# Residuals of the last two layers' weight tiles: from GpSimd and VectorE to VectorE alone

## The chip, the cores and the metric

The kernel runs on one core of a Trainium2 chip. TensorE (PE) does the matrix products, VectorE (DVE), ScalarE (ACT) and GpSimd (POOL) work on tiles, SyncE (SP) issues most of the DMAs. The metric is the device time of one execution in microseconds. Each engine carries out its own instructions in order; an instruction waits on semaphores for what it needs from another engine or a DMA.

## The reference

The input x has 256 tokens of 1024 channels. A first block (16 meta tokens in front, sliding-window attention beside a state-space model, then a feed-forward layer of 16,384 one-neuron experts) is followed by two more layers, and those are what the change touches:

```
def even_layer(x, ln, w_in, qkn, lam, subln, w_out, layer):
    h = rmsnorm(x, ln)
    aq, ak, av, az, bq, bk, bv, bz = split_cols(h @ w_in, EVEN_SPLITS)
    oa = dilated_attention(rmsnorm(heads(aq)), rmsnorm(heads(ak)), heads(av), ...)
    ob = diff_attention(rmsnorm(bq), rmsnorm(bk), heads(bv), lam_f, ...)
    mixed = concatenate([oa * silu(az), rmsnorm(ob, subln) * (1 - lam_init) * silu(bz)])
    return x + mixed @ w_out

def odd_layer(x, ln, w_in, qkn, phi_pe, phi_w1, phi_w2, w_out):
    h = rmsnorm(x, ln)
    cq, ck, cv, cz, dq, dkc, dvc, dks, dvs, dkw, dvw, dz, dg = split_cols(h @ w_in, ODD_SPLITS)
    oc = moba_attention(rmsnorm(heads(cq)), rmsnorm(heads(ck)), heads(cv), ...)
    k_cmp = rmsnorm(compress_blocks(heads(dkc), phi_pe[0], phi_w1[0], phi_w2[0]))
    v_cmp = compress_blocks(heads(dvc), phi_pe[1], phi_w1[1], phi_w2[1])
    od = nsa_attention(rmsnorm(heads(dq)), k_cmp, v_cmp, ..., sigmoid(dg), ...)
    mixed = concatenate([oc * silu(cz), od * silu(dz)])
    return x + mixed @ w_out
```

All of it is in float32.

## The kernel before, in words

Every large product is made of three products of a shorter format (fp32r), so that little precision is lost (`mm3`): a weight tile w of 128x1024 is rounded to H, its residual is Lo = w - H, and the activations are split into xH and xL in the same way. L1702 multiplies xH by H, L1703 xH by Lo, L1704 xL by H, all three into the same PSUM bank (`pr` in the last two layers, `ps` before them).

The weight tiles of the whole kernel come through one object, `Feed`. For each unit it issues the load of w on SyncE (L89, five w buffers), the rounding to H as a copy on ScalarE (L102), and the residual as a subtraction (L103) on the engine that the unit's job list names; `eng[(2 * i + q) % len(eng)]` goes through that list in turn. It stays two, later three, units ahead of the one in use. The job lists of the last two layers, `we`, `woe`, `wod`, `wog` and `woo`, have 32 + 8 + 28 + 4 + 8 = 80 units, of 1024 columns but for the four of `wog`, which have 560. Before them, in the first block, the residuals are on VectorE, but for the four of `wu`, which are on GpSimd.

`even` (L1366) and `odd` (L1433) are one `Layer` each. `enter` transposes the activations, `group` makes one slice of the projection with 4 units, 16 k-steps and two halves of the tokens. What follows a slice is `heads` for queries and keys: a square (L1192, ScalarE), a sum per head (L1193), `rstd` (L1712 to L1720, some 15 small VectorE instructions, an integer start value and three Newton steps), the scaling (L1196, L1197, into qs), and later, on TensorE, the transposes of qs (L1203). Other slices are `values` (a scaled copy) or `swish`. `scores` multiplies queries by keys (L1295), takes them with their bias from PSUM (L1298) and makes the softmax; `weigh` transposes the probabilities S (L1334) and multiplies them by the values (L1340). In `even`, two score matrices are combined (L1402) and the result is normed per head (L1417 to L1423, emx). In `odd`, keys of two kinds are normed into kn (L1470 to L1475, transposed at L1482), and a small compression (X, Y, copied over partitions by DMA at L1578, then gathered into XS at L1588) gives kr (L1630, transposed at L1639). The projection runs as a background to the attention: its matmuls are handed out in steps between the attention's.

Which instruction stands where on an engine is decided by a scheduler, which plans the whole program by its own costs and writes each engine's order. A residual's engine is one of its inputs, so the diff of one line moves instructions on several engines.

Of the kernel before, what the change touches and what calls it, by code (L numbers as in the profile page):

```python
# [1642 lines left out]
def body(tc, A, out):  # L1643
# [3 lines left out]
    with ExitStack() as ctx:  # L1647
# [23 lines left out]
        def evac(dst, src):  # L1671
# [3 lines left out]
            else:  # L1675
# [2 lines left out]
        c.evac = evac  # L1678

        P, V = nc.gpsimd, nc.vector  # L1680
        LE = [P, P, V]
        jobs = [(A["wu"], 1024, [P]), (A["wkv"], 1024, [V]), (A["wq"], 1024, [V]), (A["wo"], 1024, [V]), (A["wqy"], 1024, [V]),
                (A["ut"], 1024, [V]), (A["pv"], 1024, [V]), (A["we"], 1024, LE), (A["woe"], 1024, LE), (A["wod"][:, :2], 1024, LE),
                (A["wog"], 560, LE), (A["wod"][:, 2:], 1024, LE), (A["woo"], 1024, LE)]

# [212 lines left out]
```

## Time and profile before

| what | us |
|---|---|
| median of 3 runs (1373.74 to 1376.59) | 1375.31 |
| the profiled execution | 1379.08 |
| its span | 1377.2 |
| PE busy in the span | 1283.5 (93%) |
| DVE busy | 930.7 (68%) |
| ACT busy | 648.4 (47%) |
| POOL busy | 424.0 (31%) |

The mean granted TensorE clock was 0.958 of full speed. The last two layers begin at about 1008 us of the span and run to its end. All times of rows are us from the start of the span unless marked ns. A gap of an engine is written behind its row as [idle before <- what ended it].

### The profile page before, as it was taken

What the parts mean: (1) busy time and instruction counts of PE and PEld (TensorE: products, weight loads), DVE (VectorE), ACT (ScalarE), POOL (GpSimd) and SP (SyncE); (2) the same over time, 40 slices, a digit from 0 to 9 for tenths busy, and PEclk for the clock granted to TensorE, in tenths of its full rate; (3) what the DMA queues carried; (4) which work ended last, traced back from release to release, by engine and by line L of the source; (5) the groups of instructions that cost most, each with busy time, mean ns of one, the idle gap of its engine ahead of it and who ended that gap; (6) DMA issues with size and microseconds to landing.
All of it is one profiled execution on the core that took longest, in us unless ns stands there. A gap on an engine that the chain in (4) does not pass through costs nothing.

```text
span 1377.2 us, 21248 instructions
## 1 busy us (share of the span) xinstructions
PE 1283.5 (93%) x7816; PEld 1107.7 (80%) x7816; DVE 930.7 (68%) x2137; ACT 648.4 (47%) x1119; POOL 424.0 (31%) x257
## 2 busy tenths in 40 slices
PE   4569899999999999998999999999998989979998
PEld 4455789999999999998887888888876768756777
DVE  6963469898898666664788855555567845585734
ACT  4424345544545444444544444544554545533552
POOL 7010000477788777600000000000043426431143
PEclk9877989999999999999999999999999979997999
DMA  5359255788887777897999865665664325551231
GB/s 200 61 61 369 76 185 174 207 229 220 234 221 209 194 208 200 250 368 245 300 305 309 301 192 188 186 193 187 186 219 131 123 79 166 196 164 50 77 107 61
DMA packets 106296, 262.75 MB, mean 191 GB/s; under 512 B 31552, under 2 KB 37056, under 8 KB 103888
## 3 DMA queue, kind: packets, MB, share of 16 engines
q1 hardware_dynamic: 75280, 227.77, 52.9%
q0 software_dynamic: 21696, 16.85, 6.6%
q10 hardware_dynamic: 9216, 16.78, 3.3%
q8 instruction: 61, 1.00, 0.3%
q14 instruction: 43, 0.35, 0.1%
HBM read 232.72 MB, written 28.38 MB: 190 GB/s over the span
## 4 chain that ended last, share of the span: by engine, by line
PE 74%; DVE 11%; DMA 6%; issue 2%; ACT 1%; SPq 0%; DVEq 0%; ACTq 0%
PE ps L890 22%; PE ps L1702 10%; PE ps L1703 10%; PE ps L1704 10%; PE pr L1702 4%; PE pr L1704 4%; PE pr L1703 4%; PE m L1295 2%; DVE Lo L103 2%; DMA glu<-in_glu 2%; PE ps L1103 2%; DMA ga<-ascr 2%; PE o L1340 1%; DMA T<-kdr 1%; DVE rs L1719 1%
## 5 line engine op out<-in xcount | busy, mean ns | idle before, releaser
L102 ACT CAST H<-w 128x1024 fp32r<-128x1024 f32 (+1 forms) x370 | 386.0, 1045 | 502.4 <-PE ps L1703 211.5
L103 DVE TENSOR_TENSOR Lo<-w,H 128x1024 fp32r<-128x1024 f32 x310 | 386.0, 1246 | 171.8 <-ACT H L102 171.7
L103 POOL TENSOR_TENSOR Lo<-w,H 128x1024 fp32r<-128x1024 f32 (+1 forms) x60 | 141.8, 2367 | 626.2 <-ACT H L102 619.5
L1061 POOL DMA_INDIRECT wscr<-sent x128 | 241.0, 1883 | 225.8 <-DVE act L1038 157.0
L1702 PE MATMUL ps<-xH,H 128*128 128x256 f32 x1024 | 290.8, 284 | 0.0
L1703 PE MATMUL ps<-xL,H 128*128 128x256 f32 x1024 | 287.8, 281 | 0.0
L1704 PE MATMUL ps<-xH,Lo 128*128 128x256 f32 x1024 | 287.6, 281 | 0.0
L890 PE MATMUL ps<-H,a 128*128 128x512 f32 x1024 | 281.8, 397 | 5.3 <-ACT a L902 3.0
L890 PEld LDWEIGHTS ps<-H,a 128*128 128x128 f32 x1024 | 194.0, 190 | 51.3 <-ACT a L902 3.2
L1702 PEld LDWEIGHTS ps<-xH,H 128*128 128x128 f32 x1024 | 193.1, 189 | 0.0
L1703 PEld LDWEIGHTS ps<-xL,H 128*128 128x128 f32 x1024 | 193.1, 189 | 0.0
L1704 PEld LDWEIGHTS ps<-xH,Lo 128*128 128x128 f32 x1024 | 193.0, 188 | 0.0
L890 PE MATMUL ps<-Lo,a 128*128 128x512 f32 x512 | 161.7, 397 | 0.9 <-DVE Lo L103 0.9
L890 PEld LDWEIGHTS ps<-Lo,a 128*128 128x128 f32 x512 | 96.8, 189 | 24.5 <-DVE Lo L103 1.9
L900 DVE TENSOR_TENSOR act<-ga,act 128x256 f32<-128x256 f32 x128 | 47.4, 420 | 26.0 <-DMA ga<-ascr 25.8
L1702 PE MATMUL pr<-H,exH 128*128 128x512 f32 x128 | 54.3, 425 | 0.9 <-ACT exH L1143 0.9
L1702 PE MATMUL pr<-H,oxH 128*128 128x512 f32 (+1 forms) x128 | 52.9, 416 | 1.1 <-ACT oxH L1143 1.1
L903 DVE TENSOR_TENSOR a<-act,a 128x256 fp32r<-128x256 f32 x128 | 53.5, 419 | 0.0
L902 ACT CAST a<-act 128x256 fp32r<-128x256 f32 x128 | 51.3, 401 | 3.1 <-DMA ascr<-ga 2.1
L1704 PE MATMUL pr<-H,oxL 128*128 128x512 f32 (+1 forms) x128 | 52.6, 411 | 0.0
L1704 PE MATMUL pr<-H,exL 128*128 128x512 f32 x128 | 52.5, 410 | 0.0
L1703 PE MATMUL pr<-Lo,oxH 128*128 128x512 f32 (+1 forms) x128 | 51.9, 406 | 0.4 <-DVE Lo L103 0.4
(493 smaller groups left out, 1956.7 us busy)
## 6 DMA issues: line engine op xcount, KB each, us to landing
w<-in_ut SPq DMA_DIRECT2D x128, 512.0 KB, 4.4
w<-in_pv SPq DMA_DIRECT2D x128, 512.0 KB, 4.3
ascr<-ga ACTq DMA_DIRECT2D x64, 256.0 KB, 3.0
ga<-ascr SPq DMA_DIRECT2D x64, 256.0 KB, 5.5
w<-in_we SPq DMA_DIRECT2D x32, 512.0 KB, 3.6
w<-in_wod SPq DMA_DIRECT2D x28, 512.0 KB, 3.7
wscr<-zero POOLq DMA_DIRECT2D x4, 2048.0 KB, 30.3
w<-in_wqy SPq DMA_DIRECT2D x16, 512.0 KB, 3.5
```

What stands on the lines that cost most here:

```text
L102: self.last = self.nc.scalar.copy(H, self.loaded[u])
L103: eng.tensor_sub(Lo, self.loaded[u], H.bitcast(FT))
L890: nc.tensor.matmul(acc[2 * th + n], a[:, s], b[:, n * 512:(n + 1) * 512], start=first and e == 0, stop=last and e == 2)
L900: V.tensor_tensor(src, ga[:, blk % 2], src, op=OP.mult)
L902: copied = nc.scalar.copy(aH, src)
L903: V.tensor_sub(aL, src, aH.bitcast(FT))
L1061: ins = c.nc.gpsimd.indirect_dma_start(out=c.wscr.rearrange("i b (t o) -> (i b t) o", o=1), out_offset=bass.IndirectOffsetOnAxis(ap=t.bitc ...
L1103: nc.tensor.matmul(p[:, a * 128:(a + 1) * 128], o1[:, a], o2[:, a], start=True, stop=True)
L1295: nc.tensor.matmul(sp[:, :off + nk], q(h)[:, ts], k(h)[:, :off + nk], start=True, stop=True)
L1702: nc.tensor.matmul(o, ah, bh, start=first, stop=False)
L1703: nc.tensor.matmul(o, ah, bl, start=False, stop=False)
L1704: nc.tensor.matmul(o, al, bh, start=False, stop=last)
```

## The change

In `body`, at L1681, the list of engines for the residuals of the last two layers is shortened from three entries to one:

```
         P, V = nc.gpsimd, nc.vector
-        LE = [P, P, V]
+        LE = [V]
         jobs = [(A["wu"], 1024, [P]), ...
                 (A["ut"], 1024, [V]), (A["pv"], 1024, [V]), (A["we"], 1024, LE), (A["woe"], 1024, LE), (A["wod"][:, :2], 1024, LE),
                 (A["wog"], 560, LE), (A["wod"][:, 2:], 1024, LE), (A["woo"], 1024, LE)]
```

Of the 80 residuals 56 change from GpSimd to VectorE, three of which have 560 columns; the 24 that VectorE had stay. GpSimd keeps the four of `wu` and its other work. The scheduler writes new orders. Three places on VectorE:

In the even layer's keys, `rstd` of the second `heads` (rs_10564, made from qs_10558), between the reduction L1193 and the scaling L1197:

```order
 L1718 TENSOR_TENSOR rs_10564<-rs_10564 128x16
 L1719 TENSOR_TENSOR rs_10564<-rs_10564 128x16
+L103 TENSOR_TENSOR Lo_10606<-w_10491,H_10605 128x1024
 L1720 SCALAR_TENSOR_TENSOR rs_10564<-rs_10564 128x16
 L1718 TENSOR_TENSOR rs_10564<-rs_10564 128x16
```

A residual that GpSimd did now stands within the chain.

In the even layer's last `heads` (qs_11025, qs_11026, rs_11031), beside the norm of the second half of the tokens (bss_10934, emx):

```order
+L1193 TENSOR_REDUCE hss_11024<-qs_11025 128x8
 L1421 SCALAR_TENSOR_TENSOR bss_10934<-rs_10941,st_10706 128x4
+L1193 TENSOR_REDUCE hss_11024<-qs_11026 128x8
 L1423 TENSOR_TENSOR emx_10280<-emx_10280,bss_10934 128x512
-L1193 TENSOR_REDUCE hss_11024<-qs_11025 128x8
-L1193 TENSOR_REDUCE hss_11024<-qs_11026 128x8
 L1712 TENSOR_SCALAR rs_11031<-hss_11024 128x16
+L103 TENSOR_TENSOR Lo_11055<-w_10912,H_11054 128x1024
 L1713 TENSOR_SCALAR ri_11032<-rs_11031 128x16
-L103 TENSOR_TENSOR Lo_11055<-w_10912,H_11054 128x1024
 L1714 TENSOR_SCALAR ri_11032<-ri_11032 128x16
 L1715 TENSOR_SCALAR rs_11031<-rs_11031 128x16
```

The two reductions are earlier by one instruction of the norm, and the residual by one of rstd.

In the odd layer, the gathers XS and the norm of its keys (kss_11932, kn_11933):

```order
+L103 TENSOR_TENSOR Lo_11861<-w_11703,H_11860 128x1024
+L103 TENSOR_TENSOR Lo_11879<-w_11709,H_11878 128x1024
 L1588 COPY XS0_11888<-X_11833 128x8x15 x4
-L1588 COPY XS1_11895<-X_11844 128x8x15 x2
 L103 TENSOR_TENSOR Lo_11911<-w_11795,H_11910 128x1024
-L1588 COPY XS1_11895<-X_11844 128x8x15 x2
+L1588 COPY XS1_11895<-X_11844 128x8x15 x4
 L1460 TENSOR_SCALAR gt_11692<-pr_11815,r_11646 128x24
 L1460 TENSOR_SCALAR gt_11692<-pr_11816,r_11646 128x24
 L1470 TENSOR_REDUCE kss_11932<-kn_11933 128x8
 L1462 TENSOR_SCALAR gt_11692<-gt_11692 128x48
+L103 TENSOR_TENSOR Lo_11963<-w_11817,H_11962 128x1024
```

Two residuals now stand ahead of the gathers and one behind kss; two more stand between it and kn. On SyncE one load of a `wod` tile now goes ahead of the X copies of L1578; on GpSimd no residual of these layers is left.

## Rows read from the trace of the kernel before

**Rows 1.** Windows: stretch, us; busy us (instructions) PE, PEld, DVE, ACT, POOL; PEclk; DMA; GB/s

```profile
1008.00:1377.00 369.00, 336.01 (x1665) 260.48 (x1664) 229.77 (x646) 174.63 (x362) 141.75 (x68) 0.93 0.38 123
1049.00:1056.00 7.00, 3.44 (x16) 2.56 (x14) 4.22 (x8) 1.21 (x3) 2.34 (x1) 0.76 0.51 150
1071.00:1109.00 38.00, 29.29 (x146) 23.89 (x146) 36.13 (x87) 15.67 (x20) 16.74 (x7) 0.97 0.40 130
1111.00:1126.00 15.00, 15.00 (x50) 10.32 (x51) 6.62 (x36) 6.50 (x27) 0.00 (x0) 0.56 0.09 24
1242.00:1268.00 26.00, 26.00 (x91) 16.95 (x90) 14.53 (x73) 11.41 (x40) 4.00 (x2) 0.64 0.07 22
1276.00:1302.00 26.00, 25.08 (x150) 20.00 (x149) 23.50 (x82) 15.44 (x43) 4.74 (x2) 1.00 0.26 78
```

**Rows 2.** Timeline of PE: start, us, engine, line, operation [idle before <- releaser]

```profile
1052.81 1.51 PE L1203 MATMUL m<-cstt,qs 128*128 128x128 f32 x6 [3.56 <-DVE qs L1197]
...
1074.83 0.44 PE L1334 MATMUL m<-cstt,S 128*128 128x128 f32 x2 [2.03 <-DVE S L1402]
...
1108.58 1.94 PE L1203 MATMUL m<-cstt,qs 128*128 128x128 f32 x8 [6.69 <-DVE qs L1197]
...
1219.07 1.16 PE L1482 MATMUL m<-cstt,kn 128*128 128x128 f32 x4 [5.39 <-DVE kn L1475]
...
1239.09 0.20 PE L1639 MATMUL m<-cstt,kr 16*128 16x16 f32 x1 [3.73 <-DVE kr L1630]
```

**Rows 3.** Views of single lines on DVE: ns min/median/max, first and last start

```profile
L1719 DVE TENSOR_TENSOR rs<-rs x39: 139/174/2412, 1020.1 to 1293.3; 128x16 f32<-128x16 f32 x21, 128x2 f32<-128x2 f32 x6, 128x4 f32<-128x4 f32 x6, 128x8 f32<-128x8 f32 x3
L1193 DVE TENSOR_REDUCE hss<-qs x14: 669/677/686, 1029.7 to 1289.2; 128x8 f32<-128x512 f32 x14
L1402 DVE SCALAR_TENSOR_TENSOR S<-S,st x8: 343/410/2585, 1064.3 to 1075.1; 128x128 f32<-128x128 f32 x4, 128x256 f32<-128x256 f32 x4
L1423 DVE TENSOR_TENSOR emx<-emx,bss x2: 691/1736/2782, 1082.9 to 1099.1; 128x512 f32<-128x512 f32 x2
L1588 DVE COPY XS<-X x8: 244/358/2469, 1203.8 to 1211.0; 128x120 f32<-128x120 f32 x8
```

**Rows 4.** Timelines of POOL and DVE at 1049 us, one row of each

```profile
1049.09 2.34 POOL L103 TENSOR_TENSOR Lo<-w,H 128x1024 fp32r<-128x1024 f32 x1 [0.45 <-DVE rs L1718]
...
1049.13 2.33 DVE L1719 TENSOR_TENSOR rs<-rs 128x16 f32<-128x16 f32 x1
```

**Rows 5.** Groups of L103: from 1006 us (two), to 1006 us; busy, mean ns | idle

```profile
L103 POOL TENSOR_TENSOR Lo<-w,H 128x1024 fp32r<-128x1024 f32 x53 | 128.1, 2422 | 618.1 <-ACT H L102 611.5 <-DVE rs L1715 3.5 <-DVE x L883 2.6
...
L103 DVE TENSOR_TENSOR Lo<-w,H 128x1024 fp32r<-128x1024 f32 x23 | 36.4, 1582 | 11.6 <-ACT H L102 11.6
...
L103 DVE TENSOR_TENSOR Lo<-w,H 128x1024 fp32r<-128x1024 f32 x286 | 348.9, 1221 | 158.6 <-ACT H L102 158.5
```

**Rows 6.** Timeline of DVE in 1071 to 1109 us

```profile
1079.13 2.24 DVE L1719 TENSOR_TENSOR rs<-rs 128x4 f32<-128x4 f32 x1
...
1084.78 1.29 DVE L1712 TENSOR_SCALAR rs<-hss 128x16 f32<-128x16 f32 x1
...
1090.47 2.54 DVE L103 TENSOR_TENSOR Lo<-w,H 128x1024 fp32r<-128x1024 f32 x1
```

**Rows 7.** Timeline of DVE in the odd layer

```profile
1203.79 5.93 DVE L1588 COPY XS<-X 128x120 f32<-128x120 f32 x6 [1.85 <-DMA X<-Y]
...
1215.22 2.26 DVE L1720 SCALAR_TENSOR_TENSOR rs<-rs,ri 128x8 f32<-128x8 f32 x1
...
1234.38 2.31 DVE L1718 TENSOR_TENSOR rs<-rs 16x2 f32<-16x2 f32 x1
...
1295.21 2.37 DVE L1196 TENSOR_SCALAR hss<-rs,r 128x8 f32<-128x8 f32 x1
```

**Rows 8.** DMA issues, the page's section 6

```profile
w<-in_wod SPq DMA_DIRECT2D x28, 512.0 KB, 3.7
```

**Rows 9.** Waits of DVE from 1006 us: total us, times, longest

```profile
DVE Lo L103 <- ACT H L102: 13.2, 11, 2.7
```

More of the change, by code (lines that the diff above doesn't have):

```diff
@@ L1680, in body @@
         P, V = nc.gpsimd, nc.vector
-        LE = [P, P, V]
+        LE = [V]
         jobs = [(A["wu"], 1024, [P]), (A["wkv"], 1024, [V]), (A["wq"], 1024, [V]), (A["wo"], 1024, [V]), (A["wqy"], 1024, [V]),
```

## The prediction

> **What bounds the kernel now.** I read first the windows of the last two layers [rows 1]. From 1008 us to the end TensorE is busy in 336.0 of 369 us and VectorE in 229.8, GpSimd in 141.8. TensorE sets the time, so an edit on VectorE or GpSimd can be worth only two things: TensorE's idle time, 33 us here, and the stretches in which its granted clock is at the lower of its two levels (1.2 instead of 2.4 GHz; mean 0.93). The next view is TensorE's timeline, to see who ends its idle time [rows 2]: the five large gaps sum to 21.4 us, and every one is ended by VectorE: by qs, S, kn, kr, each the last product of a chain of small dependent instructions (rstd, lines 1712 to 1720). Why are those chains long? The line views [rows 3] answer: the multiplication L1719 takes 0.14 to 0.17 us, but up to 2.41. The timelines of both engines side by side [rows 4] show when: GpSimd's residual runs from 1049.09 for 2.34 us, VectorE's L1719 from 1049.13 for 2.33 us, and they end together. The tensor_reduce L1193, 677 ns in the median, never stretches (669 to 686). I call a VectorE instruction that is held until GpSimd's residual ends a lock.
>
> The Trainium skill says the same in "SBUF — State Buffer", section "Who interferes with whom": the port pair that the two engines share is an exclusive lock, which a reduction never takes. Another page speaks against the change: "Perfetto Trace Analysis", section "Optimizing Scalar/DVE Operations", says that moving operations between these two engines might not help because of that port. By it the sum would be near zero; it is rival B, which is priced from rows below.
>
> **The change, part by part.** Of the 80 residuals Lo of the last two layers, 56 leave GpSimd: 53 of 128x1024 and three of 128x560. GpSimd took 2.42 us for one, VectorE takes 1.22 where GpSimd is quiet, 1.58 in the last layers [rows 5]. VectorE gets 53 x 1.22 = 64.7 us more, and three small ones of about 1.22 x 560/1024 = 0.67 (an estimate), 66.7 in all. It loses its own stretching: 23 x (1.58 - 1.22) = 8.3 us on its own residuals, and the locks on the rest. GpSimd keeps 15 - 3 = 12 small instructions, so a few locks may stay. The totals decide nothing, since VectorE, at most 229.8 + 66.7 = 296.5 of 369, has room on the whole; what counts is what stands in each chain that TensorE waits for. I went through the order of the changed kernel at each place, with the durations of before.
>
> - Keys of the even layer, gap 3.56 at 1052.81 [rows 2]. The chain holds two locks, of which one stands in [rows 4]: 2 x (2.4 - 0.17) = 4.4. In the changed order one more residual stands inside it (first place in the order): +1.2. Net -3.2; the gap can lose at most its 3.56. Bounds -3.6 and +1.2.
> - Softmax to the last heads, 1071 to 1109, gaps 2.03 and 6.69 [rows 2]. VectorE is busy 36.13 of 38 us with seven GpSimd residuals in the stretch [rows 1], so here every us on VectorE is a us for TensorE. Locks: L1402's longest 2.59 - 0.41, its median, = 2.17; L1719 2.24 - 0.17 = 2.07; L1712 1.29 - 0.17 = 1.12, and a like one of 0.88; L103 2.54 - 1.22 = 1.32 [rows 6]; L1423 2.78 - 0.69 = 2.09 [rows 3, 6]; one more of that kind on L1713, 2.08. Sum 11.7. Against it ten residuals stand where three did: 7 x 1.22 = 8.5. Net -3.2. Three more TensorE matmuls now stand ahead of the transposes; at 25.08/150 = 0.17 us each [rows 1] that fills another 0.5 of the gap. So -3.7. If VectorE had no locks to lose it would be +8.5, and no more than the 8.7 of the two gaps can go: bounds -8.7 and +8.5.
> - kn in the odd layer, gap 5.39 at 1219.07. Two locks, 2.26 and its like, are 4.2; six copies XS take 5.93 where the median copy takes 0.36, 3.7 more [rows 3, 7]. In front of kn stand now five more residuals (third place in the order): 6.1, of which two fit into the 1.85 us in which VectorE waited for X [rows 7]; two of 560 columns come before those, 1.3 in all, of which I count half, 0.7, between none and all. On SyncE one weight load now goes ahead of the X copies, which can make X late by at most the 3.7 us of such a load [rows 8]; loads run side by side on 16 engines, and I take 1.0. Net -7.9 + 6.1 - 1.9 + 0.7 + 1.0 = -2.0. Bounds -5.4, the gap itself, and -7.9 + 6.1 + 1.3 + 3.7 = +3.2.
> - kr, gap 3.73 at 1239.09. Two locks, one of them the 2.31 of [rows 7]: 4.2 less, one residual more: 1.2. kr's chain now also stands ahead of the q heads'. Net -2.8. Bounds -3.7 and +1.2.
> - Odd middle, 1240 to 1302. In 1276 to 1302 VectorE is busy 23.50 of 26 and TensorE 25.08 [rows 1]: the one place where TensorE doesn't wait yet and could. Eleven residuals stand where three did, +9.8; a lock of 2.37 [rows 7], 2.2 net, its like on L1712 and a shorter one of 1.6 go, -5.9; VectorE's 2.5 us of idle time carry the most of the rest. I take +1.5; bounds 0 and +4.
>
> The gaps sum to -3.2 - 3.7 - 2.0 - 2.8 + 1.5 = -10.2.
>
> **The clock.** After the gap of 6.69 the granted clock in 1111 to 1126 is 0.56: (1 - 0.56)/0.5 x 15 = 13.2 us at the lower level, with TensorE busy all 15. After the gap of 3.56 it is 0.76 over 7 us: 3.4 us [rows 1, 2]. With the gap of 6.69 cut to about 3.0, the like of the second, I expect the short stretch in place of the long one: (13.2 - 3.4)/2 = -4.9. The third, (1 - 0.64)/0.5 x 26 = 18.7 us after the gap of 3.73, shows that a small gap can draw a long one too, so I credit nothing there; bounds 0 and -9.4.
>
> Sum: -10.2 - 4.9 = -15.1 on the profiled execution's 1379.1 (its span is 1377.2, 1.9 lies around it): 1364.0. That execution stood 0.27% above the median of the runs, 1375.31; taken down by that, 1360.
>
> **Rivals.**
> A, more of the clock. If the kr gap of under 1 us draws no lower stretch at all, 18.7/2 = 9.4 us come back there, and the 3.4 left in the first give 1.7: -26.2, a median of 1349. For it: the stretch begins with that gap. Against: the gap of 3.56 drew far less than that of 3.73, so the gap's length isn't the whole of it, and the matmuls around this one are few (91 in 26 us).
>
> B, nothing gained. VectorE gets back from the port what it spends on residuals: the chains are as long as before, the gaps and the clock stay, 1375. For it: 11.7 of locks against 8.5 of residuals in the densest stretch is a small difference of large numbers, and where GpSimd did a residual, it did it off the path. Against: at kr and at the keys the count is two locks to one residual.
>
> C, slower: residuals that wait hold VectorE's queue. GpSimd could wait for H without harm: its residuals were idle 611.5 us for ScalarE's copy [rows 5]. On VectorE, instructions go in order, and its own residuals from 1006 us waited 13.2 us in 11 waits, 0.55 per residual over 24 [rows 9]; everything queued behind one waits too, the rstd chains above all. Where VectorE is saturated that adds 10 x 0.55 = 5.5 in 1071 to 1109 and 11 x 0.55 = 6.1 in 1276 to 1302; the gaps sum to -10.2 + 11.6 = +1.4, the first lower stretch stays, and a gap of 7.6 in the odd middle draws one like that after 6.69, 13.2/2 = 6.6. Together +8.0: 1387.1, a median of 1383. It decides from about 0.5 us per residual in these two stretches. Against: in them VectorE is late itself, so that H is mostly there before its turn comes.
>
> D, that GpSimd still holds VectorE: its 12 remaining instructions fall into the chains. For two more locks, 2 x 2.2 off the gain, 1365; it lies within the forecast's range.
>
> **How the numbers follow.** Forecast 0.55 (1353 to 1369: half of the way to the bounds of its terms, D included), A 0.15, B 0.15, C 0.15. No change that this kernel's measurement can tell is within 0.2%, 1372.6 to 1378.1. Faster: 0.55 + 0.15 = 0.70; same 0.15; slower 0.15. The range leaves out most of C and the far end of A: 1346 to 1378.
>
> **What would show it.** Right: GpSimd's busy time from 1008 us on falls from 141.8 to about 10; the residuals on VectorE fall to a mean of 1.22, and L1719's longest in these layers to 0.2; the transposes L1203 wait under 1 us at the first place and about 3 at the second, L1639 about 1, L1482 about 3.5; the clock in the 15 us after the second is near 0.9. VectorE's busy time rises by less than 66.7 us, since the locks go. Wrong: a sum of VectorE's waits for H far above 13.2 (rival C); a new gap after 1276 us; gaps as large as before with VectorE full (rival B); or the kn gap above 5.4, which would put it on the X transfers behind the weight load.

## The result and the profile after

The changed kernel takes 1332.67 us (median of 4 runs, 1329.63 to 1334.54) against 1375.95 in the same comparison: a ratio of 0.9673 (95% interval 0.9650 to 0.9697), 43 us faster. 1360 was forecast, with 1346 as the lower end. The direction held; the size was nearly three times what I had worked out. Rival A (1349) was nearer and still fell short. Of all runs below, one of the changed kernel's repeat (2469.7 us) and one of `wu_v` (1349.6) stand far above the others; the ratios leave them out.

The windows of the changed kernel, columns as in [rows 1]: the last two layers, then the stretch from L1402 to the last heads, the first scores behind it, and two of the odd middle.

```profile
1002.50:1327.50 325.00, 314.82 (x1665) 246.30 (x1663) 234.80 (x701) 174.99 (x362) 14.59 (x12) 1.00 0.45 139
1059.00:1088.00 29.00, 28.79 (x144) 23.61 (x143) 28.03 (x91) 14.96 (x19) 0.00 (x0) 1.00 0.52 150
1088.00:1103.00 15.00, 15.00 (x78) 10.59 (x77) 8.37 (x40) 10.86 (x38) 0.00 (x0) 1.00 0.31 97
1203.00:1229.00 26.00, 26.00 (x131) 18.23 (x130) 21.11 (x113) 13.83 (x43) 0.00 (x0) 1.00 0.35 102
1229.00:1268.00 39.00, 39.00 (x242) 30.44 (x242) 30.44 (x111) 20.13 (x52) 0.00 (x0) 1.00 0.26 77
```

The first row, held against the first of [rows 1], gives the whole account. The stretch is 325.0 us instead of 369.0: -44.0. TensorE is busy 314.8 instead of 336.0 for the same 1665 matmuls: -21.2, and that is the clock, 1.00 instead of 0.93. The rest is TensorE's idle time, 10.2 instead of 33.0: -22.8. VectorE's busy time rose by 5.0 only, though it has some 66.7 us of new work (an estimate of the prediction): by these totals about 60 us of its busy time before were waiting. Held one by one against the median of their kind in the changed kernel, VectorE's instructions before were 52 us longer. In the second row VectorE is as full as before (28.03 of 29) and TensorE no longer waits beside it.

(The two profiled executions differ by 49.5 us, since the first block ended 5.5 us earlier in the second: TensorE's first transpose of these layers starts at 1011.1 before, at 1005.6 here, and at 1007.8 in a repeat below. The 44.0 is close to the 43 of the medians.)

What TensorE waited for in the changed kernel: total us, times, longest. In before it waited 10.5 for qs (10.25 of it in [rows 2]), 5.4 for kn, 3.7 for kr and 2.0 for S [rows 2].

```profile
PE m L1482 <- DVE kn L1475: 1.8, 1, 1.8
PE pr L1702 <- ACT oxH L1143: 1.1, 1, 1.1
PE pr L1702 <- ACT exH L1143: 1.0, 2, 0.9
PE pr L1702 <- ACT mT L1243: 0.6, 2, 0.3
PE m L1203 <- DVE qs L1197: 0.6, 3, 0.2
```

kn alone is left of the five. And VectorE's side: the line L1719 as in [rows 3], but over the whole program, the residuals from 1002 us as in [rows 5], and their wait as in [rows 9].

```profile
L1719 DVE TENSOR_TENSOR rs<-rs x57: 142/166/219, 9.3 to 1252.4; 128x16 f32<-128x16 f32 x24, 128x2 f32<-128x2 f32 x15, 128x4 f32<-128x4 f32 x6, 128x3 f32<-128x3 f32 x3
...
L103 DVE TENSOR_TENSOR Lo<-w,H 128x1024 fp32r<-128x1024 f32 x76 | 93.4, 1233 | 28.3 <-ACT H L102 28.2
...
DVE Lo L103 <- ACT H L102: 29.5, 28, 2.9
```

The longest L1719 is 0.22 us instead of 2.41: no lock is left on it. The residuals do wait for H, 29.5 us where rival C reckoned with 13.2 and 56 x 0.55 more; but the waits fall where VectorE has room (in the dense second row above it is busy 28.03 of 29 us), and no wait of TensorE for VectorE grew.

### The profile page after: what moved, and what is told of

Same layout as the page of the kernel before. It is cut to its first block, busy times and chain, and to the rows that moved or that the text cites. A ratio compares the mean times of both kernels' runs of the same rounds, so it can differ in the third digit from the quotient of the medians.

```text
span 1327.9 us, 21246 instructions
## 1 busy us (share of the span) xinstructions
PE 1260.6 (95%) x7816; PEld 1092.6 (82%) x7816; DVE 935.7 (70%) x2193; ACT 648.7 (49%) x1119; POOL 292.9 (22%) x201
## 4 chain that ended last, share of the span: by engine, by line
PE 84%; DVE 6%; ACT 2%; DMA 1%; issue 1%; DVEq 0%; SPq 0%; ACTq 0%
PE ps L890 26%; PE ps L1702 10%; PE ps L1703 10%; PE ps L1704 10%; PE pr L1702 5%; PE pr L1704 5%; PE pr L1703 5%; PE ps L1103 2%; PE m L1295 2%; DVE Lo L103 2%; PE o L1340 2%; PE m L363 1%; PE m L1334 1%; DMA ga<-ascr 1%; ACT H L102 1%
## 5 line engine op out<-in xcount | busy, mean ns | idle before, releaser
L103 DVE TENSOR_TENSOR Lo<-w,H 128x1024 fp32r<-128x1024 f32 (+1 forms) x366 | 445.2, 1218 | 186.8 <-ACT H L102 186.5
L1382 POOL TENSOR_TENSOR emx<-emx,vz 128x512 f32<-128x512 f32 x2 | 3.5, 1750 | 543.7 <-DVE vz L1228 543.7
L1090 DVE TENSOR_TENSOR o<-cstt,sel 128x512 f32<-128x512 f32 x32 | 22.1, 692 | 43.0 <-PE ps L1103 27.6
L844 ACT ACTIVATE ga<-ps 128x256 f32<-128x256 f32 x128 | 48.4, 378 | 6.7 <-PE ps L1704 5.5
L1703 PE MATMUL pr<-Lo,exH 128*128 128x512 f32 x128 | 51.4, 402 | 0.0
```

The source lines that it names most:

```text
L103: eng.tensor_sub(Lo, self.loaded[u], H.bitcast(FT))
L844: nc.scalar.activation(ga[:, blk % 2], p[:, :T], AF.Gelu)
L1703: nc.tensor.matmul(o, ah, bl, start=False, stop=False)
```

## The experiments

Three theories stood at the start. L: GpSimd's residuals lock VectorE's dependent chains, TensorE waits at their ends, and its waits draw stretches at the lower clock. O: the gain is the new order that the scheduler wrote. R: TensorE had waited for GpSimd's slower residuals themselves.

**One layer at a time.** `even_only` gives the odd layer's lists the old engines, `odd_only` the even layer's:

```
-        LE = [V]
+        LE, LO = [V], [P, P, V]
...
-                (A["wog"], 560, LE), (A["wod"][:, 2:], 1024, LE), (A["woo"], 1024, LE)]
+                (A["wog"], 560, LO), (A["wod"][:, 2:], 1024, LO), (A["woo"], 1024, LO)]
```

(`odd_only` has `LE, LO = [P, P, V], [V]`; LO goes to the first two of `wod`, too.)

> Residuals of the even layer all on VectorE, those of the odd layer as before (two of three on GpSimd). Theory L (locks): GpSimd's residuals hold VectorE's dependent chains, TensorE waits at the chain's end, and each such wait draws a stretch at the lower clock; then the gain is the sum of its places, and the even layer's places hold half: the even layer shrank by 21.6 of the 43.8 us, so 1375 - 22 = about 1353. Theory O (order): the gain comes from the new order that the scheduler wrote, whose effect need not split by layer; anything from 1335 to 1375. Theory R (lateness): TensorE waited for GpSimd's slower residuals themselves; no gap of before ends with one, so about 1375.

> The reverse: residuals of the odd layer on VectorE, those of the even layer as before. Theory L: the odd layer shrank by 22.2 us of the 43.8, so about 1353, and the two gains of this run and the last add up to that of the change. Theory O: need not add up.

Measured: 1351.1 us, ratio 0.9814 (0.9763 to 0.9864), and 1355.7, ratio 0.9820 (0.9778 to 0.9862). Each is worth about 25 us, and both times lie within 3 us of the 1353 that L gave; together 50 +- 9, against 45 by the ratio of the whole change. TensorE's gaps split by layer, too: the first two rows are waits of `even_only`, the other two of `odd_only`.

```profile
PE m L1482 <- DVE kn L1475: 5.4, 1, 5.4
PE m L1639 <- DVE kr L1630: 3.7, 1, 3.7
```

```profile
PE m L1203 <- DVE qs L1197: 10.6, 3, 6.8
PE m L1482 <- DVE kn L1475: 2.1, 1, 2.1
```

Where GpSimd still had the residuals, the gaps of before stand to a tenth of a us; where it hadn't, they are gone or, for kn, down to 2.1, as in the changed kernel. R is dead: none of these waits is for a residual. O is weakened.

**The locks put back, the order kept.** `pool_again` leaves all residuals on VectorE, and GpSimd repeats those that were its own (54 of the 56: the first two are made before the repetition is switched on) into a tile `junk`; the last line is cut out of a longer one:

```
-            eng.tensor_sub(Lo, self.loaded[u], H.bitcast(FT))
+            eng.tensor_sub(Lo, self.loaded[u], H.bitcast(FT)); self.again and self.again[u] and self.again[u](self.loaded[u], H, n)
...
+        ... (lambda wt, H, n: nc.gpsimd.tensor_sub(junk[:, :n], wt[:, :n], H[:, :n].bitcast(FT))) if (2 * i + q) % 3 < 2 else None ...
```

> The changed kernel, with all residuals on VectorE; beside it GpSimd subtracts the same tiles again, for the units that were its own, into a tile that nobody reads. VectorE's work, TensorE's work and who makes each residual are as in the changed kernel. Theory L: the locks come back and VectorE has the residuals as well, so all of the gain goes and more: 1375 to 1400. Theory O: the order on VectorE is near that of the changed kernel, 1333 to 1340. Theory R: nobody waits for GpSimd, 1333.

Measured: 1429.7 us, ratio 1.0377 (1.0340 to 1.0413): 97 us above the changed kernel, above the range that L gave. The order of TensorE, VectorE, ScalarE and SyncE is that of the changed kernel, instruction by instruction; only GpSimd's differs. So O falls as the account of the gain: the same order with GpSimd busy is slower than before. Its last layers as a window, the group of the repetition (L1778) and that of L103, and TensorE's two longest waits:

```profile
1000.00:1424.00 424.00, 353.56 (x1663) 270.67 (x1661) 321.11 (x701) 176.08 (x362) 170.58 (x66) 0.88 0.34 106
...
L1778 POOL TENSOR_TENSOR junk<-w,H 128x1024 f32<-128x1024 f32 x51 | 147.7, 2897 | 648.6 <-ACT H L102 642.5 <-issue 4.2 <-POOL junk L1778 0.8
L103 DVE TENSOR_TENSOR Lo<-w,H 128x1024 fp32r<-128x1024 f32 x75 | 130.0, 1741 | 18.7 <-ACT H L102 18.7
...
PE m L1203 <- DVE qs L1197: 23.9, 4, 6.6
PE m L1482 <- DVE kn L1475: 8.6, 1, 8.6
```

VectorE has the same 701 instructions and is busy 321.1 instead of 234.8 us: 86 us of being held. TensorE idles 70 us, its clock falls to 0.88. GpSimd pays as well, 2.90 us in the mean for a subtraction that took 2.42 [rows 5]. Not all of TensorE's waits are for chains on VectorE: 5.6 us are for two products of GpSimd's own (emx, omx).

**A quarter of each lock.** `pool_quarter` is `pool_again` with `n // 4` columns in GpSimd's repetition.

> As pool_again, but GpSimd's repeated subtraction covers a quarter of the columns: as many GpSimd instructions at the same places, each about a quarter as long (0.6 us). Theory L: a lock lasts what is left of the GpSimd instruction, so of the 97 us that pool_again cost over the changed kernel about a quarter or less is seen: 1340 to 1360. If the count of GpSimd instructions or their semaphores were the price, it would stay near 1430.

Measured: 1341.4 us, ratio 0.9736 (0.9713 to 0.9759), some 9 above the changed kernel. The number of GpSimd instructions is the same; their length is what counts. The mean was not my 0.6 us:

```profile
L1778 POOL TENSOR_TENSOR junk<-w,H 128x256 f32<-128x256 f32 x51 | 61.0, 1197 | 650.5 <-ACT H L102 637.1 <-issue 12.5 <-POOL junk L1778 0.8
```

The shortest took 0.72 us; the mean of 1.20 holds what these subtractions waited themselves. With 40% of the GpSimd time VectorE was held some 14 us instead of 86 (busy 248.5 us with the same 701 instructions), and the cost is a tenth of the 97 us.

**All on GpSimd.** `all_pool` has `LE = [P]`.

> The other end: all 80 residuals of the two layers on GpSimd. VectorE loses 24 x 1.22 = 29 us of work and meets 24 more GpSimd residuals, each of which held it about 50/56 = 0.9 us, 21 us of locks. Theory L: gaps as before or larger, since locks fall into the chains and residuals often didn't: 1370 to 1395. A theory of VectorE's load (that it simply had too much to do) says faster than before: about 1350 to 1365.

Measured: 1405.8 us, ratio 1.0197 (1.0158 to 1.0235). L's direction, 11 us over its range; the theory of VectorE's load falls outright. Its last layers:

```profile
1008.00:1405.00 397.00, 342.47 (x1664) 266.16 (x1662) 234.41 (x622) 175.04 (x362) 195.98 (x92) 0.90 0.37 114
```

VectorE, rid of all residuals of these layers, is busy 234.4 us; with all of them, in the changed kernel, 234.8. What it saved in work it spent on being held.

**A late chain, known and unknown.** `gap_ak` and `gap_kr` make a chain longer with VectorE's own work; `lock_ak` and `lock_kr` hold the same chains with GpSimd instructions.

```
-            rr = c.rstd(ss, 16, 1.0 / 64)
+            rr = c.rstd(ss, 16, 1.0 / 64); [V.tensor_tensor(qs[0], qs[0], qs[0], op=OP.max) for _ in range(10 if mark == "ak" else 0)]
```

(`gap_kr`: twenty of `V.tensor_tensor(kr, kr, kr, op=OP.max)` behind kr's rstd; `lock_ak`, `lock_kr`: `pool_again` with two subtractions for units 23 and 24, or 55 and 56, and none for the others.)

> The changed kernel with ten more VectorE instructions of 128x512 (0.69 us each, 6.9 in all) in the last heads chain of the even layer, between rstd and the scaling: a late chain without any GpSimd residual. The question is what a wait of TensorE draws by itself. Theory L with the clock following TensorE's waits: a gap of 5 to 7 us before these transposes L1203, and lower-clock stretches behind it of 3 to 17 us; 1333 + 6 + 2 to 8 = 1341 to 1347. Rival G (the clock follows GpSimd's activity, not the gap): a gap, no stretch, 1338 to 1340. Rival H (slack: the chain had that much room): no gap, 1333.

> The changed kernel with twenty more small VectorE instructions (16x128, some 0.2 us each, 4 in all) in kr's chain. Before, the gap of 3.73 us there stood at the start of 20.5 us at the lower clock. Theory L: a gap of 3 to 4 us before L1639 and a stretch of 3 to 20 us behind it: 1333 + 4 + 2 to 10 = 1338 to 1346. Rival G: 1337, no stretch. Rival H: no gap, 1333.

Measured: 1337.4 us, ratio 0.9710 (0.9689 to 0.9730), and 1336.8, ratio 0.9720 (0.9694 to 0.9746). L's gap did not come: TensorE waited neither for ak's qs nor for kr (in `gap_kr` it waited 2.4 us for another tile, sc at L1560). The scheduler knows what a VectorE instruction costs: it laid `gap_ak`'s ten between the steps of rstd, and in both kernels it moved other matmuls in front of the transposes. So these two say nothing of what a gap at these chains draws, but something else: a delay that the scheduler counts is planned around. From TensorE's first transpose in `enter` to the end, `gap_ak`'s profile takes 0.5 us more than the changed kernel's, `gap_kr`'s 3.6, with the wait of 2.4 in it. (Both medians stand 4 to 5 us above the changed kernel's, which did not run beside them; differences of that size are not read here.) Locks are not in the scheduler's count, as the next two runs show.

> The changed kernel itself, beside the next three on one chip, so that differences of a few us can be read: 1330 to 1336 on every theory.

> The changed kernel with four GpSimd subtractions that nobody reads (two for each of units 23 and 24, 2.4 us each, 9.6 in all), which run while VectorE works through the last heads chain of the even layer; the order on TensorE, VectorE and ScalarE is that of the changed kernel, instruction by instruction. Theory L with the clock following the gap: VectorE's chain is held two to four times, a gap of 4 to 8 us before the transposes, and 3 to 17 us at the lower clock behind it: 6 to 16 us above after_again. Rival G (the clock follows GpSimd's activity over the whole layer): the gap alone, 4 to 8 us.

> The same at kr's chain in the odd layer: two subtractions for each of units 55 and 56. Theory L: a gap of 3 to 7 us before L1639 and 3 to 20 us at the lower clock: 5 to 17 us above after_again. Rival G: 3 to 7. If the chain has room there: 0 to 2.

Measured on one chip: 1332.8 (ratio 0.9663, 0.9615 to 0.9710), 1344.1 (0.9742, 0.9700 to 0.9785) and 1344.2 (0.9739, 0.9690 to 0.9787). By the ratios each of the two is some 11 us above the changed kernel (the single runs of each kernel spread over 8 to 14 us, so this is good to about 5), with the order of every other engine unchanged. `lock_ak`: GpSimd's four subtractions, the four VectorE instructions that they held, the gap, and the window behind it.

```profile
1083.12 10.88 POOL L1778 TENSOR_TENSOR junk<-w,H 128x1024 f32<-128x1024 f32 x4 [507.78 <-ACT H L102]
...
1083.38 2.38 DVE L1712 TENSOR_SCALAR rs<-hss 128x16 f32<-128x16 f32 x1
...
1086.81 2.37 DVE L1713 TENSOR_SCALAR ri<-rs 128x16 int32<-128x16 int32 x1
...
1089.30 2.32 DVE L1715 TENSOR_SCALAR rs<-rs 128x16 f32<-128x16 f32 x1
...
1091.73 2.31 DVE L1719 TENSOR_TENSOR rs<-rs 128x16 f32<-128x16 f32 x1
...
1097.65 1.94 PE L1203 MATMUL m<-cstt,qs 128*128 128x128 f32 x8 [8.63 <-DVE qs L1197]
...
1098.00:1108.00 10.00, 10.00 (x50) 6.69 (x49) 7.42 (x37) 5.43 (x19) 0.00 (x0) 0.86 0.38 110
```

Four instructions of 0.17 us became 9.38 us, and the gap is 8.63. Behind it, with GpSimd quiet, the clock is 0.86 (in the repeat of the changed kernel, 1090 to 1100, 1.00). In `lock_kr` the same reads 7.71 and 0.76:

```profile
1211.45 0.26 PE L1639 MATMUL m<-cstt,kr 16*128 16x16 f32 x1 [7.71 <-DVE kr L1630]
...
1211.00:1221.00 10.00, 9.55 (x38) 6.74 (x38) 5.89 (x23) 3.04 (x5) 0.00 (x0) 0.76 0.48 150
```

In the profiles, from TensorE's first transpose in `enter` to the end, `lock_ak` takes 11.6 us more than the repeat of the changed kernel, and `lock_kr` 9.3. In `lock_kr` that is the gap and its stretch, (1 - 0.76)/0.5 x 10 = 4.8 us at the lower level, worth 2.4. In `lock_ak` the stretch behind the gap is worth 1.4, and a second one, at kn, 1.7. The gap of kn there is that of the repeat, where it drew nothing; `lock_ak` first, then the repeat:

```profile
1198.44 0.30 PE L1482 MATMUL m<-cstt,kn 128*128 128x128 f32 x1 [2.10 <-DVE kn L1475]
...
1198.00:1208.00 10.00, 9.56 (x95) 7.72 (x96) 5.42 (x16) 3.83 (x8) 0.00 (x0) 0.83 0.38 115
```

```profile
1190.03 0.30 PE L1482 MATMUL m<-cstt,kn 128*128 128x128 f32 x1 [2.08 <-DVE kn L1475]
...
1190.00:1200.00 10.00, 9.97 (x104) 7.98 (x105) 6.93 (x26) 4.87 (x9) 0.00 (x0) 1.00 0.43 119
```

So one gap of 8 us costs about 10 with the clock behind it. Rival G falls: the stretches come with GpSimd quiet. A lower stretch needs no GpSimd near it: in `odd_only`, where the odd layer has no GpSimd residual, one stands around a gap of 2.10, first the gap, then the window:

```profile
1217.44 0.30 PE L1482 MATMUL m<-cstt,kn 128*128 128x128 f32 x1 [2.10 <-DVE kn L1475]
...
1211.00:1222.00 11.00, 8.90 (x90) 7.06 (x89) 7.73 (x23) 4.16 (x7) 0.00 (x0) 0.84 0.76 229
```

But a gap does not fix its stretch. At kn the gap was 1.6 to 2.1 us in eight of the profiles, and it drew one in three of them (`lock_ak`, `odd_only`, `more_v`). The kr gap was 3.73 in `even_only` as in before, and the 26 us behind it had a clock of 0.93, not the 0.64 of [rows 1]. What decides the length of a stretch stays open.

**Going further.** `more_v` moves GpSimd's last 12 instructions of these layers (L1320, L1382, L1454, L1469) to VectorE, `wu_v` the four residuals of `wu`:

```
-        jobs = [(A["wu"], 1024, [P]), ...
+        jobs = [(A["wu"], 1024, [V]), ...
```

> The changed kernel with GpSimd's last 12 instructions of these layers on VectorE too (L1320, L1382, L1454, L1469). Theory L: what locks are left go, but VectorE has 68% more work at the kn gap (four squares, 0.8 us, stand in kn's chain, where TensorE still waits 1.8 us): 1328 to 1333. If VectorE is now full in its dense stretches: 1335 to 1340.

> The changed kernel with the first block's four residuals that are still GpSimd's on VectorE too. Theory L: four locks fewer, in a part where TensorE is idle 43 of the first 100 us for other reasons: 0 to 4 us below after_again. If VectorE's chain there is the bound, since it is busy 78 of those 100 us: up to 5 above.

Measured: 1338.2 us, ratio 0.9716 (0.9693 to 0.9739), and 1334.8, ratio 0.9664 (0.9621 to 0.9706) beside 0.9663 of the changed kernel itself. `wu_v` changes nothing that can be measured. `more_v` is no gain: L's 1328 to 1333 was missed, and the time lies in the range given for a full VectorE. But TensorE's waits are the same (kn 1.8 us), so that isn't shown, and the changed kernel did not run beside it. No version here beats the changed kernel: TensorE is busy 97% of these layers at the full clock.

## Why the prediction was wrong

The mechanism was right, down to the lines: locks on VectorE's chains, TensorE's gaps at their ends, the clock behind the gaps. Two terms of the sum were mis-sized, and the clock's was also worked out by a step that failed.

**The gaps: -10.2 forecast, -22.8 measured.** Place by place, forecast and measured: keys -3.2 and -3.4 (the gap is now 0.19); dense stretch -3.7 and about -8.5; kn -2.0 and -3.6; kr -2.8 and -3.7; odd middle +1.5 and -0.8; the rest, mostly the even layer's entry (waits for exL and oxL), which had no term, 0 and -2.8. At the keys, in the dense stretch and at kr the gap went almost whole, as far as the prediction's bounds allowed. (kr's -4.2 + 1.2 is -3.0; the -2.8 is a slip of 0.2.) The largest miss is the dense stretch. It runs from L1402 to the last qs; its ends on VectorE, before and then in the changed kernel:

```profile
1071.79 3.78 DVE L1402 SCALAR_TENSOR_TENSOR S<-S,st 128x256 f32<-128x256 f32 x4
...
1107.75 1.28 DVE L1197 TENSOR_TENSOR qs<-pr,hss 128x512 f32<-128x512 f32 x2
```

```profile
1059.19 1.67 DVE L1402 SCALAR_TENSOR_TENSOR S<-S,st 128x256 f32<-128x256 f32 x4
...
1087.39 1.28 DVE L1197 TENSOR_TENSOR qs<-pr,hss 128x512 f32<-128x512 f32 x2
```

That is 36.0 us before and 28.2 now: -7.8 instead of -3.2. Three things were wrong in that count. Nine residuals stand there, six more than before, not seven. I charged 1.22 us for each, but one that falls between two steps of a chain costs less, since each step waits for the one before it anyway:

```profile
1084.43 0.18 DVE L1719 TENSOR_TENSOR rs<-rs 128x16 f32<-128x16 f32 x1
1084.52 1.22 DVE L103 TENSOR_TENSOR Lo<-w,H 128x1024 fp32r<-128x1024 f32 x1
1085.66 0.17 DVE L1720 SCALAR_TENSOR_TENSOR rs<-rs,ri 128x16 f32<-128x16 f32 x1
1085.86 0.17 DVE L1718 TENSOR_TENSOR rs<-rs 128x16 f32<-128x16 f32 x1
1086.07 0.17 DVE L1719 TENSOR_TENSOR rs<-rs 128x16 f32<-128x16 f32 x1
```

L1719 to L1720 is 1.23 us with the residual between them, 0.21 is such a step without one: 1.02 for the residual. Six of them are 6.1 us at that price, not 8.5. The last 2 us or so I put down to the two chains rs_10891 and rs_10941, which the new order interleaves, so that the steps of one fill the waits of the other; no run tests that alone. The price of the locks was right: against the medians of the changed kernel, seven instructions of this stretch were 11.7 us longer before. At kr and kn the same lower price of a residual would apply, but it is not measured there; at the odd middle, where I feared +1.5, VectorE is busy 30.44 of 39 us with the residuals in it and TensorE 39.00.

**The clock: -4.9 forecast, -21.2 measured.** I let the first long stretch shrink and left the second, on the ground that a gap of under 1 us might still draw one. In the changed kernel's profile of these layers there is no stretch at all: the clock is 1.00 over 325 us. The failed step is that I priced each stretch from the gap that I expected to be left, so that the first error was counted twice: gaps of 0.2 us, not of 3, stand before the transposes L1203, and none at kr. The three stretches that I priced were worth 6.6, 1.7 and 9.4 us, and I credited 4.9 of the 17.7. Two more stood in before that had no term, at kn and at the even layer's entry:

```profile
1216.00:1226.00 10.00, 6.93 (x80) 5.71 (x81) 5.13 (x15) 1.31 (x3) 1.46 (x1) 0.66 0.51 159
1014.00:1022.00 8.00, 6.42 (x26) 4.74 (x26) 6.79 (x22) 4.58 (x13) 3.44 (x2) 0.79 0.75 263
```

TensorE's busy time times the share at the lower level, (1 - 0.66)/0.5 = 0.68 and 0.42, halved, is 2.4 and 1.3 us. All five add up to 21.4, against the 21.2 measured. Rival A held this mechanism with 0.15 and took it for the exception. Over all runs the mean clock was 0.951 to 0.963 before and 0.971 to 0.978 after, so it isn't one lucky profile.

**The rivals.** B (VectorE gets back what it spends) nearly held for the totals, where VectorE's busy time rose by only 5.0 us, and fell for the chains: the locks had stood within them, the residuals cost them less, and the dense stretch went from 36.0 to 28.2 us. The Trainium skill's "Perfetto Trace Analysis", section "Optimizing Scalar/DVE Operations", says that moves between the two engines might not help because of the port. Here the move towards VectorE was worth 3.3%, and the reverse cost 2.0%. By the Trainium skill's "SBUF — State Buffer", section "Who interferes with whom", the first to issue holds the port and the other engine waits out the whole instruction. `lock_ak` agrees to a tenth of a us: the last subtraction ends at 1094.00, the L1719 that it held at 1094.04. C's waits came (29.5 us) and met room on VectorE. The X transfers behind the weight load did not show: kn's gap is 1.8.

## What to carry to other kernels

Before giving an elementwise tile operation to GpSimd because VectorE looks busy, look at what VectorE's instructions last beside it: where short ones stretch to the length of GpSimd's, much of VectorE's busy time is waiting, and the total says nothing of the room that it has. When several short gaps of TensorE have one cause, price the clock also for the case in which all of them go, and not only gap by gap: here that gave 21.2 us, and gap by gap 4.9. A scheduler plans around costs that it knows; a lock isn't one of them, and falls where the plan left no room.

## What the runs showed of the hardware

- Instructions that take 0.17 us on 128x16, or 0.15 on 16x2, were held 2.3 to 2.4 us, integer tensor_scalar ones as well; tensor_reduce was not [rows 3].
- The lock works both ways: GpSimd's subtraction takes 2.42 us in the mean [rows 5] and 2.90 where VectorE also does all its residuals. In `lock_ak` one that was issued while a residual ran on VectorE took 3.35 us instead of 2.34, the shortest of the four:

```profile
1085.67 1.21 DVE L103 TENSOR_TENSOR Lo<-w,H 128x1024 fp32r<-128x1024 f32 x1
...
1085.80 3.35 POOL L1778 TENSOR_TENSOR junk<-w,H 128x1024 f32<-128x1024 f32 x1
```

- A quarter of the columns took GpSimd 0.72 us at the shortest, against 2.34 for all of them.
- One program's runs on one chip differ in their granted clock (before: 0.951 to 0.963, with 1388 and 1369 us at these ends), and the stretch behind the same gap of 3.73 us differs between two runs. A profile's lower stretches are a sample: what one gap draws can't be read from one profile.
